# Stick-breaking attention in a macaron block: transposed weights made two groups at a time, their products with v further back, and the last pairs' results and output weights handled on other queues

## The chip, the cores and the metric

One core of a Trainium2 chip runs one program. The metric is the device time of one execution in microseconds (us); the time of a kernel is the median over several runs. The core has a matrix engine (PE), with its weight loads shown apart (PEld), a vector engine (DVE), an activation engine (ACT), GpSimd (POOL), and a queue engine (SP) that here issues the DMAs. Each engine runs its own instructions strictly in the order in which they stand in the program, and waits at an instruction whose operands or buffers are not ready.

## The reference, cut to what matters

The block is: half a SwiGLU feed-forward layer, attention, half a SwiGLU layer, each on an RMS-normalised x, for 1024 frames of 1024 features. Everything in the change lies in the attention.

```python
def stick_breaking_attention(xn, w_qkv, q_gain, k_gain, w_o):
    qkv = (xn @ w_qkv).reshape(b, s, 3, SB_HEADS, SB_HEAD_DIM)      # 16 heads of 64
    q = rms_norm(qkv[:, :, 0], q_gain); k = rms_norm(qkv[:, :, 1], k_gain); v = qkv[:, :, 2]
    for blk in range(s // Q_BLOCK):                                 # 8 blocks of 128 frames
        z = einsum('bhqd,bhkd->bhqk', q[:, :, lo:hi], k[:, :, :hi]) / sqrt(SB_HEAD_DIM)
        mask = s_idx < t_idx
        log_1m = where(mask, log_sigmoid(-z), 0.0)
        rev_excl = (sum of log_1m over the later keys of the row)
        w = where(mask, exp(log_sigmoid(z) + rev_excl), 0.0)
        outs.append(einsum('bhqk,bhkd->bhqd', w, v[:, :, :hi]))
    return concatenate(outs) @ w_o
```

The frames come in reversed, so that the running product over later keys becomes a scan from left to right.

## The kernel before, in words

The program has three long stretches: the first feed-forward layer, the attention with its output projection, and the second feed-forward layer. Matrix products in full precision are made as three products of a high and a low part (`mm3`, lines L308 to L310: high by high, high by low, low by high). A tensor is split into its two parts by `split`: ACT copies the high part out (L196), and DVE, or POOL where a caller says so, subtracts it from the tensor to get the low part (L197).

The attention works on eight pairs of heads (`p` = 0 to 7), which follow each other in time. While a pair is worked on, the q, k and v of the next pair are computed as filling work (`qkv`, 24 steps of nine or six matmuls with 384 columns into the PSUM banks `bq`). For a head `hd` and a half of the frames (`half` 1 is blocks 4 to 7, `half` 0 blocks 0 to 3) there are two kinds of work:

- `scores(state, hd, half)`: for each block `tb` of 128 query frames and each half `kb` of the keys, two matmuls make z in one of three banks `bz` (L1058), ACT takes two sigmoids from it (L1062), DVE runs a scan over one of them, which gives the running product (L1066), and POOL multiplies the scan into the other (L1073). The result is a tile w (`w03` is head 0, block 3 of its half). A bank `bz` comes free when its scan has read it. `prep_q` and `prep_k`, which turn q and k (L1016) and split them (L1020, L1021), use the same three banks.
- `values(state, p, hd, half)`: w is needed with the keys on the partitions. For each group (a block `sb` of 128 keys; the last group holds two blocks) `turn` transposes up to four 128 x 128 pieces of w into one of two banks `bt` (L1095), and `split` takes them out into a tile `th` (ACT) and a tile `tl` (DVE), of which there are two each. `apply` then multiplies v by `th` and by `tl` into the bank `bo` (L1113). A bank `bt` comes free when `tl` is written, a slot of `th` and `tl` when its product has read it. There are three groups for half 1 and seven for half 0. After the last group the sum is taken out into the tile `o`; after the second head, pairs 0 to 6 split `o` into two tiles `w12` and `w13`, store both to DRAM (`o_keep`, L1127), and `load_o` brings them back into `xh` and `xl` once the x that these hold is no longer read; pair 7 writes into `xh` and `xl` at once.

A pair's time is cut into four parts, a, b, c and d. The table `UNITS` says which scores a part makes, and `BEFORE` which earlier scores it applies: part a scores head 1 half 1 and applies head 0 half 1; b scores head 0 half 0 and applies head 1 half 1; c scores head 1 half 0 and applies head 0 half 0; d scores the next pair's head 0 half 1 and applies head 1 half 0.

The order on the engines comes from a list `plan` of (time, function). The times are the author's own units, used for sorting only; the functions are called in that order, and each call gives its instructions the next priorities. A scheduler that knows which instructions wait for which then lays out each engine's fixed order by priority, and can put a ready instruction ahead of one that it expects to wait. Before, group i of a part with `span` units was turned at

```python
t = TURN + (span - TURN) * i / len(groups)        # TURN = 4.0
put(part, t, to_turn)
put(part, t + APPLY, to_apply)                    # APPLY = 2.3
```

In the last pair there is no next qkv. Its place is taken by `project`: parts of the output projection for the first half of the columns (table `SHARES`, matmuls named `bq<-raw,xh` and the like). The weights w_o come in two halves of four loads each (`out_weights`, L1248): the loads go to two `raw` tiles in turn, so a load waits until the tile's earlier content is split. Which engine subtracts is set by `ON_POOL` for the first half (`wo0` to `wo2` POOL, `wo3` DVE); the second half was all on DVE.

Of the kernel before, what the change touches and what calls it, by code (L numbers as in the profile page):

```python
# [17 lines left out]
P = 128  # L18
# [15 lines left out]

ON_POOL = {"wo0", "wo1", "wo2"}

# [17 lines left out]

TURN, APPLY = 4.0, 2.3
RAW = 6
# [57 lines left out]
def macaron_kernel(ctx, tc, x, g1, w1_in, w1_out, gm, w_qkv, gq, gk, w_o, g2, w2_in, w2_out, out):  # L114
# [801 lines left out]
    with ExitStack() as stack:  # L916
# [121 lines left out]
        def scores(state, hd, half):  # L1038
# [3 lines left out]
            def step(tb, kb):  # L1042
# [29 lines left out]
                c1 = max(c0, 1)  # L1072
                pool_e.tensor_tensor(wt[:, c1 : c0 + n], wt[:, c1 : c0 + n], om[:, c1 - 1 : c0 + n - 1], op=ALU.mult)  # L1073

            return [partial(step, tb, kb) for tb in range(half * 4, half * 4 + 4) for kb in range(half, 2)]

        def values(state, p, hd, half):
# [5 lines left out]
            def blocks(sb):  # L1083
                return min(4, sb - tb0 + 1)

            def turn(sbs):
                w = state["w", hd, half]
                tp = bank("bt")
                n = 0
                for sb in sbs:  # L1090
                    for i in range(max(blocks(sb), 2)):
                        c = (sb - tb0 - i) * P

                        src = w[tb0 + i][:, c : c + P] if i < blocks(sb) else first[:, P : 2 * P]
                        pe.transpose(tp[:, n : n + P], src, ident)  # L1095
                        n += P
                th, tl = now[sbs] = [pl["th"].tile([P, NHALF], F32R, name=n) for n in ("th", "tl")]
                split(tp[:, :n], th[:, :n], tl[:, :n])

            def apply(sbs):  # L1100
# [18 lines left out]
                dve.tensor_tensor(o[own, :], ot[own, :], o[own, :], op=ALU.add)  # L1119
                if hd == 1 and p < NP - 1:  # L1120

                    oh, ol = (
                        pl["w"].tile([P, T - i * P], F32R, name=f"w1{i}", bufs=1)[:, :NHALF] for i in (2, 3)
                    )
                    split(o, oh, ol)
                    for to, src in zip(o_keep, (oh, ol)):
                        sp.dma_start(to[rows(p), HALVES[half]], src.bitcast(F32))  # L1127
                elif hd == 1:
                    split(o, xh[:, p, HALVES[half]], xl[:, p, HALVES[half]])
# [4 lines left out]
        def load_o(half):  # L1134

            for i in range(NP - 1):
                for to, src in zip((xh, xl), o_keep):
                    sp.dma_start(to[:, i, HALVES[half]].bitcast(F32), src[rows(i), HALVES[half]])


        states = [{} for _ in range(NP)]
# [35 lines left out]
        for p in range(-1, NP):  # L1177
# [9 lines left out]
            for part, span in PARTS.items():  # L1187
# [3 lines left out]
                if this is not None:  # L1191
                    groups = values(this, p, *BEFORE[part])
                    for i, (to_turn, to_apply) in enumerate(groups):
                        t = TURN + (span - TURN) * i / len(groups)
                        put(part, t, to_turn)
                        put(part, t + APPLY, to_apply)
            if nxt is not None:
                if p >= 0:
                    fills = qkv(p + 1, nxt)
                    for part, span in PARTS.items():  # L1200
                        for i in range(FILLS[part]):
                            put(part, (span - (3.0 if part == "d" else 0.0)) * (i + 0.5) / FILLS[part], fills.pop(0))
                put("c", 15.0, partial(prep_q, nxt, 1))
                put("c", 17.5 if p >= 0 else 20.0, partial(prep_k, nxt, 0, 1))
                put("d", 8.0, partial(prep_k, nxt, 1, 1))
            if this is not None:
                put("a", 5.0, partial(prep_q, this, 0))
                put("a", 7.5, partial(prep_k, this, 0, 0))
                put("b", 8.0, partial(prep_k, this, 1, 0))
            if 0 <= p < NP - 2:  # L1210
# [30 lines left out]
    with pools(*PROJECTION) as pl:  # L1241
# [3 lines left out]
        def out_weights(c, k, rooms):  # L1245
# [7 lines left out]
            if c is HALVES[0] and k < 6:  # L1253

                there = seen[:, k // 2 : k // 2 + 1] if k < 4 else wo[-1][1][:, 0:1].bitcast(F32)
                pool_e.tensor_tensor((l_ if k < 4 else h_)[:, 0:1], there, there, op=ALU.mult)
            split(raw, h_, l_, lane(f"wo{k // 2}") if c is HALVES[0] else dve)
            return [(h_[:, s], l_[:, s]) for s in HALVES]
# [108 lines left out]
```

## Time and profile before

| | us |
|---|---|
| median of 3 runs (lowest to highest) | 1930.62 (1930.38 to 1931.1) |
| the profiled execution | 1931.22 |
| its span in the trace | 1929.4 |
| PE busy | 1906.1 (99% of the span) |
| PEld, DVE, ACT, POOL busy | 1623.1, 1237.0, 978.5, 1115.7 |
| attention with its qkv and the first part of the projection | about 686 to 1240 of the span |
| mean granted PE clock | 1.0 of full speed |

How to read it: matmuls overlap, since the next one starts while the last one drains, and the ends in the trace are modelled. So "busy" hides short waits of PE. What a wait costs is read from the starts: the distance from one matmul's start to the next one's, less the usual distance for that size. Times are counted from the start of the span. Idle time on an engine that nobody waits for costs nothing.

### The profile page before, as it was taken

The numbers are of one execution on the slowest core, as the hardware profiler recorded it, in microseconds if no ns is written. First come the engines' busy times: TensorE is split into PE (matmuls) and PEld (weight loads), VectorE is DVE, ScalarE is ACT, GpSimd is POOL, SyncE is SP. The second block draws the span as 40 slices with busy tenths as digits, with TensorE's granted clock in tenths as the row PEclk, the third lists the DMA queues.
The fourth block names the chain that finished last, engine by engine and source line by source line (L and its number), as shares of the span: only waits on it lengthen the run. The fifth ranks groups of instructions, "written<-read, shape, count | busy, mean of one in ns | idle before, by whom it ended". The sixth has DMA issues, their size and how long they took to land.

```text
span 1929.4 us, 26653 instructions
## 1 busy us (share of the span) xinstructions
PE 1906.1 (99%) x9362; PEld 1623.1 (84%) x9362; DVE 1237.0 (64%) x1714; ACT 978.5 (51%) x1794; POOL 1115.7 (58%) x994
## 2 busy tenths in 40 slices
PE   9999999999999999999999999999999999999999
PEld 8878888888888899898989897788888888888887
DVE  6855455536775667887787778477455545548645
ACT  6433433343335467777787777344433443334332
POOL 5766667656456646655665564114667667655554
PEclk9999999999999999999999999999999999999999
DMA  6233323238996401111101144511323323369973
GB/s 202 88 120 105 104 87 126 94 118 294 347 321 234 134 25 45 39 39 45 45 31 48 50 143 141 197 55 59 116 88 125 100 97 104 121 212 341 336 268 139
DMA packets 169558, 259.70 MB, mean 135 GB/s; under 512 B 11728, under 2 KB 82384, under 8 KB 169424
## 3 DMA queue, kind: packets, MB, share of 16 engines
q1 hardware_dynamic: 169280, 258.00, 39.2%
q8 instruction: 73, 1.20, 0.3%
q14 instruction: 61, 0.50, 0.1%
q10 hardware_dynamic: 144, 0.00, 0.0%
HBM read 197.66 MB, written 60.29 MB: 134 GB/s over the span
## 4 chain that ended last, share of the span: by engine, by line
PE 85%; DVE 7%; ACT 2%; POOL 2%; issue 2%; DMA 1%; SPq 0%; DVEq 0%; POOLq 0%; ACTq 0%
PE ka L308 6%; PE ka L310 6%; PE ka L309 6%; PE kc L308 4%; PE kc L310 4%; PE kc L309 4%; PE bq L309 4%; PE bq L308 4%; PE bq L310 4%; PE kb L308 4%; PE ma L309 4%; PE ma L310 4%; PE kb L310 4%; PE ma L308 4%; PE kb L309 4%; PE bo L1113 3%
## 5 line engine op out<-in xcount | busy, mean ns | idle before, releaser
L197 POOL TENSOR_TENSOR rp<-raw,rp 128x1024 fp32r<-128x1024 f32 x84 | 212.5, 2534 | 169.9 <-ACT rp L196 159.1
L197 POOL TENSOR_TENSOR u<-sf,u 128x512 fp32r<-128x512 f32 x160 | 227.4, 1423 | 136.4 <-ACT u L196 136.4
L197 POOL TENSOR_TENSOR u<-raw,u 128x512 fp32r<-128x512 f32 x128 | 186.2, 1457 | 157.9 <-ACT u L196 157.1
L196 ACT ACTIVATE u<-sf 128x512 fp32r<-128x512 f32 x160 | 100.8, 630 | 204.9 <-PE kb L309 86.9
L1073 POOL TENSOR_TENSOR w<-w,om 128x512 f32<-128x512 f32 (+4 forms) x128 | 140.8, 1104 | 110.2 <-DVE om L1066 83.9
L446 DVE TENSOR_TENSOR h<-h 128x512 f32<-128x512 f32 x110 | 135.4, 1235 | 85.7 <-POOL h L554 85.0
L196 ACT ACTIVATE rp<-rh 128x1024 fp32r<-128x1024 f32 (+1 forms) x78 | 76.5, 984 | 196.6 <-PE mb L309 59.2
L308 PE MATMUL bq<-wqh,xh 128*128 128x384 f32 x512 | 174.5, 341 | 0.0
L310 PE MATMUL bq<-wqh,xl 128*128 128x384 f32 x512 | 172.2, 336 | 0.0
L309 PE MATMUL bq<-wql,xh 128*128 128x384 f32 x512 | 172.0, 336 | 0.0
L576 DVE TENSOR_TENSOR raw<-raw 128x1024 f32<-128x1024 f32 (+1 forms) x60 | 89.9, 1500 | 109.8 <-DMA raw<-w_out 94.9
L196 ACT ACTIVATE u<-raw 128x512 fp32r<-128x512 f32 x128 | 80.3, 630 | 151.6 <-PE ka L309 100.9
L308 PE MATMUL ka<-xh,u 128*128 128x512 f32 x352 | 137.2, 390 | 1.9 <-ACT s L499 1.9
L308 PE MATMUL ma<-rp 128*128 128x512 f32 x352 | 137.0, 389 | 0.0
L310 PE MATMUL ka<-xh,u 128*128 128x512 f32 x352 | 137.0, 389 | 0.0
L310 PE MATMUL ma<-rp 128*128 128x512 f32 x352 | 136.9, 389 | 0.0
L309 PE MATMUL ka<-xl,u 128*128 128x512 f32 x352 | 136.9, 389 | 0.0
L309 PE MATMUL ma<-rp 128*128 128x512 f32 x352 | 136.9, 389 | 0.0
L1062 ACT ACTIVATE w<-bz,f 128x512 f32<-128x512 f32 (+2 forms) x192 | 112.7, 587 | 42.2 <-PE bz L1058 39.4
L554 POOL TENSOR_TENSOR h<-h,g 128x512 f32<-128x512 f32 x80 | 112.9, 1411 | 35.4 <-DVE h L503 33.6
L475 DVE TENSOR_TENSOR sf<-raw 128x512 f32<-128x512 f32 x80 | 80.3, 1003 | 77.9 <-POOL u L197 77.9
L197 DVE TENSOR_TENSOR rp<-rh,rp 128x1024 fp32r<-128x1024 f32 (+1 forms) x70 | 110.8, 1600 | 22.1 <-ACT rp L196 19.6
(309 smaller groups left out, 5497.1 us busy)
## 6 DMA issues: line engine op xcount, KB each, us to landing
raw<-w_out SPq DMA_DIRECT2D x120, 512.0 KB, 5.7
raw<-w_in SPq DMA_DIRECT2D x86, 512.0 KB, 3.6
k<-h SPq DMA_DIRECT2D x154, 256.0 KB, 2.1
rh<-k SPq DMA_DIRECT2D x64, 512.0 KB, 6.3
raw_qkv<-w_qkv SPq DMA_DIRECT2D x64, 192.0 KB, 3.0
x_keep<-x SPq DMA_DIRECT2D x32, 256.0 KB, 3.7
x<-x_keep SPq DMA_DIRECT2D x32, 256.0 KB, 5.4
raw<-w_out SPq DMA_DIRECT2D x24, 256.0 KB, 3.6
```

Of the source, the lines that this page charges most:

```text
L196: first = act.activation(hi, raw, AF.Copy).ins
L197: return first, (engine or dve).tensor_tensor(lo, raw, hi.bitcast(F32), op=ALU.subtract).ins
L308: pe.matmul(dst, ah, bh, start=start and i == 0, stop=False, skip_group_check=onto)
L309: pe.matmul(dst, ah, bl, start=False, stop=False, skip_group_check=onto)
L310: pe.matmul(dst, al, bh, start=False, stop=stop and i == n - 1, skip_group_check=onto)
L446: dve.tensor_tensor(src, hb[of[0]], hb[of[1]], op=getattr(ALU, of[2]))
L475: dve.tensor_tensor(f[n], x, y, op=op)
L554: pool_e.tensor_tensor(h, h, gs[k], op=ALU.mult)
L576: dve.tensor_tensor(w[0], w[0], w[1], op=getattr(ALU, W_OF[m][2]))
L1062: marks["scored"] = act.activation(to, z, AF.Sigmoid, scale=state["f", half][:, sign, tb % 4, hd : hd + 1]).ins
L1073: pool_e.tensor_tensor(wt[:, c1 : c0 + n], wt[:, c1 : c0 + n], om[:, c1 - 1 : c0 + n - 1], op=ALU.mult)
L1113: pe.matmul(ot[:, :n], vv, t[:, c : c + n], start=start, stop=stop)
```

## The change

It leaves every product and its operands as they were, and moves work in order and between engines and queues:

- `TURN` becomes a number per part (a 4.0, b 4.0, c 7.5, d 5.0), `APPLY` 3.3 where it was 2.3, and the groups are turned in twos: groups 0 and 1 at one time, 2 and 3 at the next.
- All transposes of a group get the priority of its first one, so that they stay together where they are ready.
- In parts c and d of the last pair `turn` and `apply` are given a priority 12 later.
- `prep_k` for head 1 half 0 moves from 8.0 to 10.7 of part b, and the last qkv step of part a comes 0.1 earlier.
- The store of `o` needs one `w` tile (`w13`) and no longer two: the low part is written over `o` itself. Pair 6 stores half 1 only; its half 0 goes into `xh` and `xl` at once, and `load_o` fetches six rows, not seven, for half 0.
- `wo3` is subtracted on POOL. For the second half of w_o the copies on ACT follow the last sigmoid that was emitted, and the subtractions are cut in two halves of 512 columns; of its four loads the first two are subtracted on POOL, behind the last product of w (`marks["weighed"]`), the other two on DVE.

```diff
-ON_POOL = {"wo0", "wo1", "wo2"}
+ON_POOL = {"wo0", "wo1", "wo2", "wo3"}
-TURN, APPLY = 4.0, 2.3
+TURN, APPLY = {"a": 4.0, "b": 4.0, "c": 7.5, "d": 5.0}, 3.3
 ...
             def turn(sbs):
-                n = 0
+                n, now_at = 0, tc.cur_priority
 ...
+                        tc.cur_priority = now_at
                         pe.transpose(tp[:, n : n + P], src, ident)
 ...
-                if hd == 1 and p < NP - 1:
-                    oh, ol = (
-                        pl["w"].tile([P, T - i * P], F32R, name=f"w1{i}", bufs=1)[:, :NHALF] for i in (2, 3)
-                    )
+                if hd == 1 and (p < NP - 2 or p == NP - 2 and half):
+                    oh = pl["w"].tile([P, T - 3 * P], F32R, name="w13", bufs=1)[:, :NHALF]
+                    ol = o.bitcast(F32R)
 ...
-            for i in range(NP - 1):
+            for i in range(NP - 2 + half):
 ...
+        def behind(f, n=12):
+            with sooner(-n):
+                f()
 ...
-                        t = TURN + (span - TURN) * i / len(groups)
+                        t = TURN[part] + (span - TURN[part]) * (i - i % 2) / len(groups)
+                        if p == NP - 1 and part in "cd":
+                            to_turn, to_apply = partial(behind, to_turn), partial(behind, to_apply)
 ...
-                put("b", 8.0, partial(prep_k, this, 1, 0))
+                put("b", 10.7, partial(prep_k, this, 1, 0))
 ...
-            split(raw, h_, l_, lane(f"wo{k // 2}") if c is HALVES[0] else dve)
+            if c is HALVES[0]:
+                split(raw, h_, l_, lane(f"wo{k // 2}"))
+            else:
+                with following(marks["scored"] if k < 4 else None):
+                    act.activation(h_, raw, AF.Copy)
+                with following(marks["weighed"] if k < 4 else None):
+                    for s in HALVES:
+                        engine = pool_e if k < 4 else dve
+                        engine.tensor_tensor(l_[:, s], raw[:, s], h_[:, s].bitcast(F32), op=ALU.subtract)
```

The order on the engines, at three places. First, ACT at the start of part c of a middle pair (`th` is the high part of a turned group, `w` and `bz` after L1062 are the two sigmoids of a score; the 128x384 score is that of block 1). Before:

```order
L980 ACTIVATE sq<-bq 128x256
L981 ACTIVATE qk_9888<-bq 128x256
L984 ACTIVATE vst<-bq 128x2x64
L196 ACTIVATE th<-bt 128x512 x2
L207 ACTIVATE rs_a<-ssq 128x16
L1062 ACTIVATE w_10279<-bz,f_9833 128x384
L1062 ACTIVATE bz<-bz,f_9833 128x384
L196 ACTIVATE th<-bt 128x512
L1062 ACTIVATE w_10279<-bz,f_9833 128x512
```

The same place after the change:

```order
L984 ACTIVATE vst<-bq 128x2x64
L1062 ACTIVATE w_10248<-bz,f_9834 128x384
L1062 ACTIVATE bz<-bz,f_9834 128x384
L207 ACTIVATE rs_a<-ssq 128x16
L196 ACTIVATE th<-bt 128x512 x2
L1062 ACTIVATE w_10248<-bz,f_9834 128x512
L1062 ACTIVATE bz<-bz,f_9834 128x512
L196 ACTIVATE th<-bt 128x512 x2
```

The first two groups now stand behind the first score of block 1, where they stood ahead of it, and the next two stand together. On PE their transposes stand nine qkv matmuls and that score further back.

Second, PE in part a of a middle pair (`bo` is the product with v, `bt` a transpose, `bz<-ident,qk` the turning of k, `bz<-kh_s` a score). Before:

```order
L1113 MATMUL bo<-th,vst 128x512
L1113 MATMUL bo<-tl,vst 128x512
L1016 MATMUL bz<-ident,qk_9446 128x128 x4
L1095 MATMUL bt<-ident,w_9657 128x128
L1095 MATMUL bt<-ident,w_9705 128x128
L1095 MATMUL bt<-ident,w_9657 128x128
L1095 MATMUL bt<-ident,first 128x128
L1113 MATMUL bo<-th,vst 128x384
L1113 MATMUL bo<-tl,vst 128x384
L1058 MATMUL bz<-kh_s_9736,q_s_9563 128x256
L1058 MATMUL bz<-kl_s_9737,q_s_9563 128x256
L308 MATMUL bq<-wqh,xh 128x384
```

The same place after the change:

```order
L1113 MATMUL bo<-th,vst 128x512
L1113 MATMUL bo<-tl,vst 128x512
L1113 MATMUL bo<-th,vst 128x384
L1113 MATMUL bo<-tl,vst 128x384
L1016 MATMUL bz<-ident,qk_9417 128x128 x4
L1098 MATMUL bt<-ident,w_9650 128x128
L1098 MATMUL bt<-ident,w_9698 128x128
L1098 MATMUL bt<-ident,w_9650 128x128
L1098 MATMUL bt<-ident,first 128x128
L308 MATMUL bq<-wqh,xh 128x384
L309 MATMUL bq<-wql,xh 128x384
L310 MATMUL bq<-wqh,xl 128x384
```

The two products with v follow each other, and the score of 256 columns that stood right behind them now stands behind nine qkv matmuls; the product of the third group stands behind that score, the first score of part b and nine more.

Third, POOL where pair 7 begins (`wd` and `wc` are the low parts of the last two loads of the first half of w_o, the rest are the products of w of blocks 5, 6 and 7). Before:

```order
L1073 TENSOR_TENSOR w_12234<-w_12234 128x383
L197 TENSOR_TENSOR wd<-raw,wa 128x1024
L1071 MEMSET w_12296 128x1
L1073 TENSOR_TENSOR w_12296<-w_12296 128x255
L1071 MEMSET w_12359 128x1
L1073 TENSOR_TENSOR w_12359<-w_12359 128x127
```

The same place after the change:

```order
L1073 TENSOR_TENSOR w_12221<-w_12221 128x383
L197 TENSOR_TENSOR wd<-raw,wa 128x1024
L197 TENSOR_TENSOR wc<-raw,wb 128x1024
L1071 MEMSET w_12281 128x1
L1073 TENSOR_TENSOR w_12281<-w_12281 128x255
L1071 MEMSET w_12344 128x1
L1073 TENSOR_TENSOR w_12344<-w_12344 128x127
```

The subtraction `wc` has come from DVE and stands ahead of the products of blocks 6 and 7. The four halves of `wf` and `wh` have come too; they stand behind the last product of pair 7.

More of the change, by code (lines that the diff above doesn't have):

```diff
@@ L1072, in step @@
                 c1 = max(c0, 1)
-                pool_e.tensor_tensor(wt[:, c1 : c0 + n], wt[:, c1 : c0 + n], om[:, c1 - 1 : c0 + n - 1], op=ALU.mult)
+                marks["weighed"] = pool_e.tensor_tensor(
+                    wt[:, c1 : c0 + n], wt[:, c1 : c0 + n], om[:, c1 - 1 : c0 + n - 1], op=ALU.mult
+                ).ins
             return [partial(step, tb, kb) for tb in range(half * 4, half * 4 + 4) for kb in range(half, 2)]
@@ L1201, in macaron_kernel @@
                         for i in range(FILLS[part]):
-                            put(part, (span - (3.0 if part == "d" else 0.0)) * (i + 0.5) / FILLS[part], fills.pop(0))
+                            t = (span - (3.0 if part == "d" else 0.0)) * (i + 0.5) / FILLS[part]
+                            put(part, t - 0.1 if (part, i) == ("a", FILLS["a"] - 1) else t, fills.pop(0))
                 put("c", 15.0, partial(prep_q, nxt, 1))
```

## The prediction, as it went on record

> **What bounds the kernel now.** I read the head of the page first, then the chain that ended last, then the busy time by stretches, then who PE waited for, and last the rows of PE in one pair.
>
> ```profile
> span 1929.4 us, 26653 instructions
> PE 85%; DVE 7%; ACT 2%; POOL 2%; issue 2%; DMA 1%; SPq 0%; DVEq 0%; POOLq 0%; ACTq 0%
> ```
>
> PE holds 85% of the chain. So time comes back only where PE stands still. The stretches (length, then busy time and count of PE, PEld, DVE, ACT and POOL, the clock, the DMA share) show where that can be: 686 to 1125 holds pairs 0 to 6, 1125 to 1240 the last of pair 6 and pair 7.
>
> ```profile
> 686.00:1125.00 439.00, 431.14 (x2599) 397.92 (x2598) 346.40 (x666) 342.71 (x749) 250.65 (x382) 1.00 0.13 41
> 1125.00:1240.00 115.00, 109.28 (x584) 89.56 (x583) 84.78 (x137) 71.04 (x141) 49.29 (x69) 1.00 0.46 151
> ```
>
> PE idles 7.9 us in the first and 5.7 us in the second, and DVE and ACT have about a fifth of their time free in the first (346 and 343 of 439), so neither is a second bound there. The 13.6 us are the least that the waits cost, since a modelled end covers the start of each wait. Who is waited for, from 684 to 1236 (total, times, longest):
>
> ```profile
> PE bt L1095 <- POOL w L1071: 4.7, 8, 0.6
> ...
> PE bz L1058 <- DVE w L1066: 2.4, 8, 1.1
> ...
> PEld bo L1113 <- DVE tl L197: 14.6, 41, 1.2
> ```
>
> Three kinds recur: a transpose that waits for POOL's product of w, a score that waits for its bank `bz`, and a product with v that waits for `tl`. The change touches all three.
>
> **Part c: the first transposes.** In each of seven pairs the chain goes from PE to a product on POOL and back; the first and the last:
>
> ```profile
> 731.34 1.63 POOL w L1073
> ...
> 1124.37 1.64 POOL w L1073
> ```
>
> One of them on PE:
>
> ```profile
> 993.86 0.49 PE L1095 MATMUL bt<-ident,w 128*128 128x128 f32 x3
> 994.99 0.77 PE L1095 MATMUL bt<-ident,w 128*128 128x128 f32 x5 [0.64 <-POOL w L1071]
> 995.51 0.42 PE L1058 MATMUL bz<-kh_s,q_s 128*128 128x384 f32 x1
> ```
>
> Transposes start about 0.11 apart (five in the 0.52 to the score). Three starting at 993.86 end their steps at 994.19; the fourth, which reads the last block's w, starts at 994.99. The cost is 0.80 (the 0.64 shown and what the modelled end hides). In the new order these transposes stand nine qkv matmuls and a score of 384 columns later, 1.9 us by the steps below, over twice the wait. The scores ahead of them don't move, so POOL's product doesn't come later. Gain 7 x 0.80 = 5.6.
>
> **Part a: bank and `tl`.** The rows of PE of one pair:
>
> ```profile
> 1037.28 0.41 PE L1113 MATMUL bo<-tl,vst 128*128 128x384 f32 x1
> 1037.84 0.39 PE L1058 MATMUL bz<-kh_s,q_s 128*128 128x256 f32 x1 [0.15 <-DVE w L1066]
> 1038.06 0.28 PE L1058 MATMUL bz<-kl_s,q_s 128*128 128x256 f32 x1
> 1038.18 0.34 PE L308 MATMUL bq<-wqh,xh 128*128 128x384 f32 x1
> 1038.36 0.34 PE L309 MATMUL bq<-wql,xh 128*128 128x384 f32 x1
> ...
> 1039.86 0.40 PE L1058 MATMUL bz<-kh_s,q_s 128*128 128x512 f32 x1
> 1040.54 0.39 PE L1113 MATMUL bo<-tl,vst 128*128 128x256 f32 x1 [0.28 <-DVE tl L197]
> 1040.76 0.28 PE L1113 MATMUL bo<-th,vst 128*128 128x256 f32 x1
> ...
> 1042.81 0.39 PE L1058 MATMUL bz<-kh_s,q_s 128*128 128x512 f32 x1
> 1043.04 0.40 PE L1058 MATMUL bz<-kl_s,q_s 128*128 128x512 f32 x1
> ```
>
> Usual steps from start to start: 384 columns 0.18, 256 columns 0.12, 512 columns 0.23. Here 1037.28 to 1037.84 is 0.56, 0.38 too long; the next step 0.22, 0.10 too long (PE starts again slowly after a wait); 1039.86 to 1040.54 is 0.68, 0.45 too long; the next 0.10 again. Together 1.03. In the new order the score of 256 columns comes nine qkv matmuls (1.6) later, and the product that waited for `tl` comes behind that score, one of 512 columns and nine more qkv matmuls: 1.6 + 0.2 + 0.5 + 1.6 = 3.9 behind its transposes. These now stand two products ahead of 1037.28, so `tl` needs some 3.5 (to 1040.54). Both waits are covered, the second by 0.4. Six pairs: 6.2.
>
> **The end of part b, and the other waits for `tl`.**
>
> ```profile
> 1054.32 0.28 PE L1113 MATMUL bo<-th,vst 128*128 128x256 f32 x1
> 1054.59 0.38 PE L1113 MATMUL bo<-tl,vst 128*128 128x256 f32 x1
> 1054.81 0.28 PE L1113 MATMUL bo<-th,vst 128*128 128x256 f32 x1
> ...
> 1003.16 0.40 PE L1113 MATMUL bo<-th,vst 128*128 128x512 f32 x1
> 1003.51 0.51 PE L1113 MATMUL bo<-tl,vst 128*128 128x512 f32 x1
> ```
>
> 0.27 and 0.22 stand where 0.12 is usual: 0.25 lost. The turning of k (four transposes) and a score of 512 columns come between, 0.9 more, so seven pairs give 1.8. In part c 1003.16 to 1003.51 is 0.12 too long. Of the 41 waits for `tl` thirteen are counted above; I take 25 of the others (the rest is the last pair's) at 0.12, 3.0, with nothing and 0.23 (a restart of 0.11 with each) as ends, 0 to 5.8. They go because a product now follows its transposes 3.3 units later in the plan and not 2.3.
>
> **What two at a time costs.** There are two banks `bt` and two slots of `th` and `tl`. A second two can be turned while the first two wait for their products, but not taken out.
>
> ```profile
> 1033.18 0.60 PE L1095 MATMUL bt<-ident,w 128*128 128x128 f32 x4
> ...
> 1033.88 0.60 ACT L196 ACTIVATE th<-bt 128x512 fp32r<-128x512 f32 x1
> ...
> 1035.16 0.67 DVE L197 TENSOR_TENSOR tl<-bt,th 128x512 fp32r<-128x512 f32 x1
> ...
> 1020.55 1.62 ACT L948 ACTIVATE wqh<-raw_qkv 128x768 fp32r<-128x768 f32 x2
> ```
>
> ACT starts 0.70 after the first of four transposes, takes 0.6, DVE 0.67. Part d is tightest: its third two needs the banks of the second two, whose `th` waits for the first two's products to have read their slots. From the start of the first group's product with `tl`: 0.4 until it is read, 0.6 and 0.7 for ACT and DVE, some 0.2 of handing over, 1.9; 0.6 more for the second group, 2.5. PE has until then that product (0.2), the next two (0.5), nine qkv matmuls (1.6) and a score (0.2), 2.5 to the first four transposes and 0.4 more to the next: margins of 0.6 and 0.4. ACT's two copies (1.62 together) stand just ahead in its order; they start 1.3 before the slot comes free, so they could eat 0.3 of it. I charge 0.2 per pair, 1.3 in all; ends 0 and 1.6 per pair (both copies late). Elsewhere at least 1.6 of qkv work lies between. The transposes' new priority, the qkv step 0.1 earlier and `prep_k` later cost nothing by themselves: no product is added, and `prep_k`'s bank has a score's whole time (1.6 of qkv) to come free. The store of `o` has as many DMAs as before, and SP loses one fetch and one store pair in pair 6; nothing on PE reads those rows that early.
>
> **The last pair.** It has little filling work, so DVE and POOL count. From the chain (start, length), then rows of PE, then of POOL:
>
> ```profile
> 1156.08 2.31 DVE wc L197
> ...
> 1172.62 1.21 DVE wf L197
> ...
> 1192.83 0.72 DVE wh L197
> ```
>
> ```profile
> 1158.28 0.48 PE L1113 MATMUL bo<-th,vst 128*128 128x512 f32 x1
> 1159.62 0.51 PE L1113 MATMUL bo<-tl,vst 128*128 128x512 f32 x1 [0.86 <-DVE tl L197]
> ...
> 1214.16 0.27 PE L1095 MATMUL bt<-ident,w 128*128 128x128 f32 x1
> 1215.67 0.33 PE L1095 MATMUL bt<-ident,w 128*128 128x128 f32 x1 [1.23 <-POOL w L1073]
> ```
>
> ```profile
> 1154.90 2.40 POOL L197 TENSOR_TENSOR wd<-raw,wa 128x1024 fp32r<-128x1024 f32 x1 [1.56 <-issue]
> ...
> 1159.07 0.72 POOL L1073 TENSOR_TENSOR w<-w 128x255 f32<-128x255 f32 x1 [1.73 <-DVE w L1066]
> ```
>
> Three subtractions for w_o lie on the chain on DVE and leave it. `wc` holds up `tl`: 1159.62 less 1158.28 is 1.34, 1.11 too long. `wf` and `wh` give 1.21 and 0.72 of chain. Part d's first transposes stand still for 1.51 less 0.11, 1.40; they move behind more projection work. Sum 4.4. Against it: `wc` on POOL ends at 1154.90 + 2.40 + 2.40 = 1159.7, 0.6 after the product of block 6 begins now, so that is 0.6 later. And at the end, where no qkv work is left and four groups stand in a row, each two can wait for slots: by the 1.9 and 2.5 above against some 1.6 of projection work, 0.3 to 0.9; I take 1.0 with a restart. Net gain 2.8. The ends are a loss of 2.4 (below), and 10.5: the 5.7 idle and 0.16 hidden in each of some 30 waits.
>
> The Trainium skill's "GPSIMD Engine Reference", section "Engine selection", says that elementwise work with two inputs belongs on VectorE, since GpSimd is about twice as slow. The rows agree for the length: 2.40 on POOL, 1.21 for `wf` on DVE. By that rule alone moving these three would be a mistake; yet `wc` took 2.31 on DVE while POOL ran `wd`, and it is the queue that counts.
>
> **The sum.** 5.6 + 6.2 + 1.8 + 3.0 - 1.3 + 2.8 = 18.1. The profiled execution took 1931.2 (1.8 around its span), 0.6 above the median shown; 1930.6 - 18.1 gives 1912.5, and I say 1912.
>
> **The rivals.**
> - POOL becomes the bound of the last pair (chance 0.20). `wc`'s 2.4 lie wholly ahead of the products of blocks 6 and 7, and nothing that leaves DVE helps PE. For it: PE does wait for POOL there (1.23 above), and POOL's chain into part b has no filling work. Against: block 6's product waits 1.73 for DVE now. Then the last pair loses 2.4 and the other pairs keep 15.3: 1917.7. This is what the skill's rule would give.
> - Waits only change their place (0.08): scores come no earlier, and what PE saves at a transpose it stands before the next scan. Against: DVE and ACT have a fifth of their time free. Between 1927 and 1934, 1930.5.
> - Slower (0.06): in parts c and d the two slots don't come free in time, because ACT's copies of the qkv weights stand ahead of `th`. With 1.6 at three double turns a pair that is 4.8 against the 2.3 that a pair gains (15.3 over six and a half): + 2.5 x 6, 1945. It decides from 0.29 at each of the eight double turns of a pair.
>
> **How the numbers follow.** The forecast has 0.66. Its own range, from the ends above, is 1902 (all waits for `tl` with restarts, 2.8 more, and the last pair's 10.5 where 2.8 are counted) to 1921 (1.6 per pair in part d and not 0.2). POOL's case lies in it and reaches 1922.5 if the waits for `tl` worth 3.0 and 1.8 stay. I give 1902 to 1923; two in ten lie outside: the last two rivals and ends of the others. About 0.2%, 3.9 us, is what a measurement of this kernel can tell from none. Faster: 0.66 + 0.20 = 0.86; same 0.08; slower 0.06.
>
> **What would show it.** Right: the seven POOL products leave the chain and PE's waits for POOL's w fall from 8 to one or two; PE's waits for `bz` go except at pair 0's start; PEld's waits for `tl` fall from 41 to under 15; PE's idle time from 686 to 1125 falls from 7.9 to under 2.5; a pair takes about 63.2 us, where POOL's rows on the chain now stand 65.5 apart (1124.37 less 731.34, by six). Wrong: PE waits for `bt` behind DVE's `tl` in part d, or the last 115 us get longer with POOL's `wc` or a raw w_o load on the chain.

## The result, and the profile after

The changed kernel takes 1914.43 us (median of 5 runs, 1914.03 to 1914.58) against 1931.1 (1930.38 to 1931.55) of the kernel before on the same chip: 16.7 us less, a ratio of 0.9913 with a 95% interval of 0.9900 to 0.9927. The forecast was 1912 (1902 to 1923). It is 2.4 above the forecast, and the sum of 18.1 us was 1.4 too large; the terms of that sum were further off than the sum, as the parts below show.

The head of the page and the chain of the changed kernel: POOL's share of the chain fell from 2% to 1%, and of the seven products of w on POOL that stood in it from 731 to 1125 us, 1.63 each, none is left.

```profile
span 1912.5 us, 26698 instructions
PE 86%; DVE 8%; ACT 3%; issue 1%; POOL 1%; DMA 0%; SPq 0%; DVEq 0%; ACTq 0%; POOLq 0%
```

Busy time by stretches (length, then PE, PEld, DVE, ACT, POOL, clock, DMA share, GB/s). The first row is the stretch that the forecast named. The second starts 13 us earlier than the forecast's second stretch, at about the same place of the work; the last product with v, which began at 1232.7, now begins at 1217.5, so the row holds some more of what follows:

```profile
686.00:1125.00 439.00, 435.45 (x2658) 408.47 (x2657) 354.52 (x687) 352.21 (x768) 260.49 (x395) 1.00 0.15 47
...
1112.00:1227.00 115.00, 112.83 (x607) 94.79 (x606) 83.24 (x139) 72.62 (x144) 61.18 (x76) 1.00 0.49 162
```

PE stands idle for 3.6 us where it was 7.9, and for 2.2 where it was 5.7. Who it waits for, from 684 to 1236 us (total, times, longest), PE first, then its weight loads:

```profile
PE bz L1058 <- DVE kl_s L1021: 1.5, 7, 0.2
PE bz L1016 <- POOL w L1071: 0.9, 1, 0.9
PE bz L1058 <- DVE w L1066: 0.9, 3, 0.3
PE bo L1116 <- DVE tl L197: 0.6, 1, 0.6
...
PE bt L1098 <- POOL w L1073: 0.2, 1, 0.2
...
PEld bo L1116 <- DVE tl L197: 6.8, 22, 1.0
PEld bz L1058 <- DVE kl_s L1021: 3.7, 7, 0.5
PEld bq L308 <- DVE f L1003: 3.4, 7, 0.5
```

The eight waits of transposes for POOL's product are down to one of 0.2, those for `bz` from 8 to 3, those for `tl` from 41 to 22. Two rows were not there before: seven times, once in each pair, a score waits for `kl_s` and a qkv matmul for `f`.

To say where the time went I use ACT's copies `kh_s`, of which each pair has four, always at the same places of the work. Four of them are shown: the first of all, the one in part a of pair 0, that in part a of pair 5, and the last one in part c of pair 6, which lies 16 us behind the 1125 us of the forecast. Before, then after:

```profile
694.83 0.69 ACT L1020 ACTIVATE kh_s<-bz,gk_sb 128x512 fp32r<-128x512 f32 x1 [2.67 <-PE bz L1016]
711.47 0.69 ACT L1020 ACTIVATE kh_s<-bz,gk_sb 128x512 fp32r<-128x512 f32 x1
1038.19 0.69 ACT L1020 ACTIVATE kh_s<-bz,gk_sb 128x512 fp32r<-128x512 f32 x1
1141.06 0.69 ACT L1020 ACTIVATE kh_s<-bz,gk_sb 128x512 fp32r<-128x512 f32 x1 [0.55 <-PE bz L1016]
```

```profile
693.68 0.69 ACT L1020 ACTIVATE kh_s<-bz,gk_sb 128x512 fp32r<-128x512 f32 x1 [2.67 <-PE bz L1016]
710.25 0.69 ACT L1020 ACTIVATE kh_s<-bz,gk_sb 128x512 fp32r<-128x512 f32 x1
1027.72 0.69 ACT L1020 ACTIVATE kh_s<-bz,gk_sb 128x512 fp32r<-128x512 f32 x1
1128.39 0.69 ACT L1020 ACTIVATE kh_s<-bz,gk_sb 128x512 fp32r<-128x512 f32 x1 [0.17 <-PE bz L1016]
```

A fifth of the stretch from the second row to the third is the period of a pair: 65.34 before, 63.49 after. From the first row to the last ("the pairs" from here on) is 446.2 and 434.7, so 11.5 us came from there. From the last row to the end of the span (1929.4 and 1912.5) is 788.3 and 784.1: 4.2 came from the end of pair 6 and from pair 7. The spans differ by 16.9, and the remaining 1.2 lie ahead of the first row, where no work was changed; that row stands between 693.4 and 695.0 in all fourteen kernels, so I take it for the spread of single executions. The same numbers for every kernel:

| kernel | period | the pairs | from there to the end | median |
|---|---|---|---|---|
| before | 65.34 | 446.2 | 788.3 | 1931.1 |
| turning edits only | 63.94 | 436.1 | 786.3 | 1918.56 |
| output-weight edits only | 65.70 | 447.9 | 788.6 | 1929.7 |
| part c's turn later only | 65.19 | 444.9 | 786.8 | 1927.29 |
| store edits only | 65.03 | 444.8 | 789.1 | 1929.57 |
| c's turn and every product later only | 64.48 | 443.5 | 789.5 | 1928.0 |
| turning and store | 63.53 | 435.0 | 785.5 | 1916.52 |
| turning and output weights | 64.05 | 436.8 | 784.6 | 1917.33 |
| after | 63.49 | 434.7 | 784.1 | 1914.43 |
| after, one group at a time | 63.77 | 437.2 | 784.2 | 1916.78 |
| after, part c's turn at 4.0 again | 64.16 | 439.6 | 783.6 | 1918.52 |
| after, part b's first score later | 63.62 | 436.1 | 784.1 | 1914.69 |
| the same, and b's first products later | 63.03 | 431.4 | 784.3 | 1911.9 |
| the same, and one fill of part c later | 62.93 | 430.7 | 784.0 | 1910.57 |

The kernel before had medians of 1930.4 to 1931.1 beside these runs, so differences of medians between groups of runs carry up to 0.7 us. The stretches of the table don't carry that, but each is of one profiled execution: for the output-weight edits it was the longest of ten (1932.37), and one wait of 2.1 for a store, 1.1 in the kernel before, is in its pairs. What PE lost in the pairs, by cause, is worked out from all its rows there: each step from start to start, less the usual one (0.11 for a transpose; 0.12, 0.17 and 0.23 for 256, 384 and 512 columns), put down to what the late instruction, or its weight load, waited for, with the slow step behind it counted to the same cause (us). The row of `tl` has many short waits; counting only those that made PE late by over 0.03 gives 0.4 to 1.2 less in it:

| PE waits for | before | c later only | after | singles | c at 4.0 | b's score | b's products | c's fill |
|---|---|---|---|---|---|---|---|---|
| POOL's w (`bt`) | 5.9 | 0 | 0 | 0 | 0 | 0 | 0 | 0 |
| DVE's w (`bz`) | 5.4 | 5.6 | 1.1 | 1.1 | 1.1 | 1.1 | 1.1 | 1.1 |
| `tl` | 9.6 | 14.0 | 4.0 | 4.5 | 10.7 | 8.3 | 4.0 | 5.6 |
| `kl_s` | 0 | 0 | 3.4 | 3.3 | 3.4 | 0 | 0 | 0 |
| `f` | 0 | 0 | 2.3 | 4.4 | 0 | 2.4 | 2.3 | 0 |
| all, with the small ones | 24.5 | 23.5 | 13.4 | 15.8 | 17.6 | 14.8 | 10.1 | 9.4 |

(In columns from the left: the kernel before, the run with c's turn alone, the changed kernel, and it with one group at a time, with c at 4.0, and the three steps of the last part of the experiments.)

### The profile page after: what moved, and what is told of

It reads as the page before. It is cut to its first block, busy times and chain, and to the rows that moved or that the text cites. A ratio compares the mean times of both kernels' runs of the same rounds, so it can differ in the third digit from the quotient of the medians.

```text
span 1912.5 us, 26698 instructions
## 1 busy us (share of the span) xinstructions
PE 1897.4 (99%) x9362; PEld 1624.8 (85%) x9362; DVE 1237.0 (65%) x1713; ACT 979.9 (51%) x1794; POOL 1127.8 (59%) x999
## 4 chain that ended last, share of the span: by engine, by line
PE 86%; DVE 8%; ACT 3%; issue 1%; POOL 1%; DMA 0%; SPq 0%; DVEq 0%; ACTq 0%; POOLq 0%
PE ka L308 6%; PE ka L309 6%; PE ka L310 6%; PE bq L308 4%; PE bq L309 4%; PE bq L310 4%; PE kc L308 4%; PE kc L309 4%; PE kc L310 4%; PE ma L310 4%; PE ma L309 4%; PE ma L308 4%; PE kb L308 4%; PE kb L309 4%; PE kb L310 4%; PE mb L310 3%
## 5 line engine op out<-in xcount | busy, mean ns | idle before, releaser
L576 DVE TENSOR_TENSOR raw<-raw 128x1024 f32<-128x1024 f32 (+1 forms) x60 | 95.0, 1585 | 105.4 <-DMA raw<-w_out 91.7
L1062 ACT ACTIVATE w<-bz,f 128x512 f32<-128x512 f32 (+1 forms) x192 | 113.1, 589 | 34.5 <-PE bz L1058 33.4
```

The source lines that it names most:

```text
L576: dve.tensor_tensor(w[0], w[0], w[1], op=getattr(ALU, W_OF[m][2]))
L1062: marks["scored"] = act.activation(to, z, AF.Sigmoid, scale=state["f", half][:, sign, tb % 4, hd : hd + 1]).ins
```

## The experiments: parts of the change alone

**The turning edits alone**, in the kernel before (every hunk of the diff on `TURN`, `APPLY`, `turn`, `behind`, the twos, the qkv step and `prep_k`; none on the store and the output weights).

> The kernel before with the turning edits alone (TURN by part, APPLY 3.3, groups in twos, transposes kept together, prep_k of part b later, the last pair's c and d put back); stores and output weights as before. Theory, the waits of PE inside the pairs are what the change removes: 1915 to 1918, the seven waits of 0.8 us for POOL's product in part c gone, most of the gain of 16.7 here. Rival, the gain comes from DVE's and SP's relief in the last pair: above 1924.

1918.56 us (1917.85 to 1919.19), ratio 0.9936 (0.9921 to 0.9951). The theory's range was missed by half a microsecond; the rival's was not reached. So 12.0 of 16.7 us are the turning's. No run tried the smaller turning edits singly: the transposes kept together, `prep_k` later, the qkv step earlier, the last pair's priorities.

**The output-weight edits alone**: `ON_POOL` with `wo3`, `marks["weighed"]` and the split cut in halves.

> The kernel before with the output-weight edits alone (wo3 subtracted on POOL, the second half cut in two, its first two loads on POOL behind the last product of w). Theory, the subtractions on DVE's queue were on the chain of the last pair: 2 to 3 us less, 1928 to 1929, the wait of 1.1 us for tl at 1159 gone. Rival, POOL becomes late for its products of w: 2.4 us more, 1933 or above.

1929.7 us (1928.93 to 1932.37), ratio 0.9996 (0.9986 to 1.0005): no change that can be measured, and neither the theory's time nor the rival's. The wait that the theory named did go: at its place the product with `tl` starts 0.32 behind the one with `th` (1159.19 and 1159.51), where it was 1.34. But the stretch behind the pairs is no shorter (788.6 against 788.3), so what it gained was lost again there; where, no run here tried.

**The turn of part c alone:**

```diff
-TURN, APPLY = 4.0, 2.3
+TURN, APPLY = {"a": 4.0, "b": 4.0, "c": 7.5, "d": 4.0}, 2.3
-                        t = TURN + (span - TURN) * i / len(groups)
+                        t = TURN[part] + (span - TURN[part]) * i / len(groups)
```

> The kernel before with one number changed: the groups of part c are turned from 7.5 and not from 4.0; APPLY 2.3 and one group at a time as before. Theory, the wait for the last block's product is simply a too early place: 7 x 0.8 = 5.6 us less, 1925 to 1926. Rival, the seven groups crowded into the rest of part c wait for their banks and tl instead: 1930 or more, with more waits of PEld for tl than 41.

1927.29 us (1926.99 to 1928.52), ratio 0.9984 (0.9975 to 0.9993): 3.3 us, of which the pairs hold 1.3. The waits for POOL's product are gone, 5.9 us, as expected, but those for `tl` grew from 9.6 to 14.0. PE in one pair now reads

```profile
998.32 0.28 PE L1058 MATMUL bz<-kl_s,q_s 128*128 128x256 f32 x1
998.44 0.34 PE L308 MATMUL bq<-wqh,xh 128*128 128x384 f32 x1
999.44 0.51 PE L1113 MATMUL bo<-tl,vst 128*128 128x512 f32 x1 [0.66 <-DVE tl L197]
999.79 0.34 PE L309 MATMUL bq<-wql,xh 128*128 128x384 f32 x1
```

998.44 to 999.44 is 1.00 where a step of 384 columns takes 0.18: 0.82 lost, as much as the 0.80 that part c's transposes had lost. The transposes moved nearer to the product that reads them, and the wait moved from the one to the other.

**The store edits alone** (one tile `w13`, the low part over `o`, pair 6's half 0 not stored).

> The kernel before with the edits of the store of o alone (one w tile, the low part over o itself, pair 6's half 0 straight into xh). Theory: within 1 us of before, 1930 to 1931.5; only the one longer wait of part a at 905.7 (1.3 where the others have 0.4) shrinks, since there a score waited for a store to leave its w tile. Rival, the stores hold up part a in every pair: 3 us less or more.

1929.57 us (1929.01 to 1930.52), ratio 0.9994 (0.9985 to 1.0003): 1.0 less than the kernel before beside it, at the edge of the theory's "within 1 us" and 0.4 below its range. The one wait that the theory named went. In the kernel before, ACT once stands, at the turn from pair 2 to pair 3, for a tile that a store still reads:

```profile
905.59 0.47 ACT L1062 ACTIVATE w<-bz,f 128x256 f32<-128x256 f32 x1 [1.76 <-DMA o_keeph<-w]
```

From part a of pair 2 to part a of pair 3 that kernel takes 66.53 us, for the pairs on both sides 65.2 and 65.0; with the store edits it takes 65.16. The second `w` tile held for the store was worth 1.3 us, once.

**Part c's turn and every product later**, one group at a time: the diff of the last but one with 3.3 in place of 2.3.

> The kernel before with two numbers alone: part c's first turn at 7.5 and every product 3.3 behind its turn in place of 2.3; one group at a time. Theory: the run with c's turn alone lost its gain since the first product of part c then stood too close behind its split (0.8 us of waiting for tl in each pair, from none); with the product one step further back that wait goes, and the pair falls from 65.0 to 64.2 or less: 1920 to 1923. Rival: with one group at a time the products only meet tl's split later in the queue of DVE, and nothing is gained over the late turn alone: 1926 to 1928.

1928.0 us (1925.2 to 1929.5 in 11 runs), ratio 0.9985 (0.9976 to 0.9994). The waits for `tl` went as the theory said, from 14.0 with the late turn alone to 3.6. Four of the six steps from pair to pair come near to its 64.2 (64.1 to 64.6), but the time does not follow: from part a of pair 5 to that of pair 6 it is 68.8 us, and there are new waits for `q_s` (4.6) and `f` (4.4). PE stands for 3.3 us at one place in pair 5, and the rows say why:

```profile
1088.72 1.06 ACT L196 ACTIVATE raw<-raw 128x1024 fp32r<-128x1024 f32 x1 [3.05 <-DMA raw<-w_o]
...
1090.31 0.45 PE L1113 MATMUL bo<-th,vst 128*128 128x384 f32 x1 [3.11 <-ACT th L196]
```

ACT takes its work in order, stood 3.05 us at the first split of w_o for the load, and the copy `th` that PE needed was behind it. A second loss lies behind the pairs, in a stretch of 789.5 where the late turn alone has 786.8: there PE once stands 2.1 us for the turning of q and k, which waits for POOL, where that run stands 0.5. So what the later products gained is given back at these two places and in the new waits. The run's wide spread fits a wait for a DMA, though no run here tried that.

## The experiments: the changed kernel with one part undone

**One group at a time:**

```diff
-                        t = TURN[part] + (span - TURN[part]) * (i - i % 2) / len(groups)
+                        t = TURN[part] + (span - TURN[part]) * i / len(groups)
```

> The changed kernel with its groups turned one at a time again (the times of part c, of part d, the products 3.3 behind, the last pair's priorities and the other edits stay). Theory, from the kernel with the turning edits alone (1918.6, where turning part c later alone gave 3.3 of 12 us) : it is the turning by twos that removes the waits of the products for tl, since two groups' splits then lie behind eight transposes and a fill; without it the PE rows of bo waiting for tl come back in parts a to d, about 0.5 to 0.9 us a pair: 1918 to 1921. Rival: the later product (3.3 in place of 2.3) does this alone, and the twos are worth nothing: 1913.5 to 1915.5.

1916.78 us (1916.5 to 1917.03): 2.35 more than with twos, between the two theories. At one product in a pair the wait for `tl` is 0.27, and the wait for `f` takes 0.63 with the step behind it where it took 0.31:

```profile
992.75 0.40 PE L1116 MATMUL bo<-th,vst 128*128 128x512 f32 x1
993.25 0.50 PE L1116 MATMUL bo<-tl,vst 128*128 128x512 f32 x1
...
994.26 0.40 PE L1058 MATMUL bz<-kl_s,q_s 128*128 128x512 f32 x1
995.01 0.44 PE L308 MATMUL bq<-wqh,xh 128*128 128x384 f32 x1 [0.36 <-DVE f L1003]
```

So the twos, which the change is named after, are worth 2.35 of its 16.7 us by the medians, 2.5 by the pairs; the waits for `tl` stay away without them (4.5 against 4.0), so it is the later products, with the rest of the turning, that removed these. What the twos took away is about half of the wait for `f` (4.4 against 2.3).

**Part c's turn at 4.0 again:**

```diff
-TURN, APPLY = {"a": 4.0, "b": 4.0, "c": 7.5, "d": 5.0}, 3.3
+TURN, APPLY = {"a": 4.0, "b": 4.0, "c": 4.0, "d": 5.0}, 3.3
```

> The changed kernel with part c's first turn at 4.0 again, as in the kernel before. Theory: part c's first transposes wait for POOL's product again, 0.8 us in each of 7 pairs as in the kernel before: plus 5.6, 1919 to 1921, with seven rows of PE bt waiting for POOL w. Rival, from the run in which the late c alone gave 3.3 us because the products behind it then waited 0.8 for tl: the place of the turn trades one wait for another, and the change of c's time is worth 0 to 3: 1914 to 1917.5.

1918.52 us (1918.36 to 1918.63), 4.1 more, nearest to the theory's number, with another wait than the theory's. No row of transposes waiting for POOL came back: POOL starts the product 1.22 ahead of the first transpose here (921.51 and 922.73) and not 0.59 as in the kernel before (928.10 and 928.69), and takes 1.29 for it and not 1.63. So the other edits cover that wait even without the later turn. PE waits 0.72 at a product with v instead, here with DVE's rows behind it:

```profile
925.54 0.40 PE L1116 MATMUL bo<-th,vst 128*128 128x512 f32 x1
926.49 0.50 PE L1116 MATMUL bo<-tl,vst 128*128 128x512 f32 x1 [0.55 <-DVE tl L197]
```

```profile
924.04 1.28 DVE L1066 TENSOR_TENSOR_SCAN om<-bz,om,first 128x512 f32<-128x512 f32 x1
...
925.75 0.68 DVE L197 TENSOR_TENSOR tl<-bt,th 128x512 fp32r<-128x512 f32 x1
```

`tl` stands on DVE behind a scan of 1.28 and two small steps, in one unbroken row. Together with the run that moved c's turn alone this is the main finding: the same edit is worth 1.3 us in the pairs of the kernel before and 4.9 in those of the changed one. It pays there only where the products stand far enough back. That alone is not enough: with the later products but none of the other edits the late turn gained nothing more (1928.0). The medians differ less, 3.3 and 4.1, since behind the pairs the late turn gains 1.5 in the one kernel and loses 0.5 in the other.

**Turning and store; turning and output weights**, each in the kernel before.

> The kernel before with the turning edits and the store edits, without those of the output weights. The turning edits alone gave 1918.6 and a steady pair of 63.84 us, all edits together 1914.4 and 63.50. Theory: the 0.3 us a pair is the store's (the split of o in place frees its buffers sooner and changes the order of DVE at the end of part a), the rest, near 1.9, is the output weights' in the last pair: pair of 63.5, 1916 to 1917. Rival: the store is worth nothing here either, as it was alone (1 us): 1918 to 1919.

> The kernel before with the turning edits and those of the output weights, without the store's. Theory: pair of 63.84 as with the turning alone, and some 1.9 us less in the last pair, where the splits of the output weights leave the queues of DVE: 1916 to 1917. Rival: the output weights alone gave 0.9 us and are worth no more here: 1917.5 to 1919.

1916.52 us (1916.49 to 1917.26) and 1917.33 (1917.17 to 1918.58). The first came as its theory said, with a period of 63.53. So the output weights are worth 2.1 us in company (1916.52 less 1914.43), 1.4 of it behind the pairs. The second lies 0.3 above its theory's range and 0.2 below its rival's, so it decides for neither. By it the store is worth 2.9 in company (1917.33 less 1914.43), 2.1 of it in the pairs. Alone the two gave 0.9 and 1.0, which can't be told from nothing.

## The experiments: where the rest of the pair's waits went

**Part b's first score behind the next fill.** In the changed kernel PE waits for `kl_s`, then starts slowly:

```profile
965.43 0.40 PE L1058 MATMUL bz<-kh_s,q_s 128*128 128x512 f32 x1
966.03 0.50 PE L1058 MATMUL bz<-kl_s,q_s 128*128 128x512 f32 x1 [0.20 <-DVE kl_s L1021]
966.37 0.34 PE L308 MATMUL bq<-wqh,xh 128*128 128x384 f32 x1
```

965.43 to 966.03 is 0.37 too long, the next step 0.11. The edit:

```diff
+                    steps = scores(state, *UNITS[part])
+                    if part == "b":
+                        put(part, 1.2, steps[0])
+                        steps = steps[1:]
-                    spread(scores(state, *UNITS[part]), start[part], start[part] + span, 0.5)
+                    spread(steps, start[part] + (span / 8 if part == "b" else 0.0), start[part] + span, 0.5)
```

> The changed kernel with the first score step of part b put behind the qkv fill that follows it (nine matmuls of 128x384, some 1.57 us) in place of ahead of it; nothing else moves in the order of PE. Theory: the 0.37 + 0.11 us that PE waits there in each of 7 pairs for the copy kl_s go (it is 0.48 late, the fill covers 1.57) and no other wait takes their place: minus 3.4, 1910.5 to 1911.5. Rival: the scores of part b come 1.6 later to ACT, POOL and DVE, and the turns of part c wait for them instead: 1914 to 1917.

1914.69 us (1914.45 to 1915.56), the time that the rival gave, though not at its place. The seven waits for `kl_s` are gone, and each pair has a new one of 0.42 at part b's first products (`tl` from 4.0 to 8.3), not at part c's turns:

```profile
904.42 0.69 ACT L1062 ACTIVATE w<-bz,f 128x512 f32<-128x512 f32 x1 [1.43 <-PE bz L1058]
```

```profile
909.28 1.15 DVE L197 TENSOR_TENSOR tl<-bt,th 128x512 fp32r<-128x512 f32 x2
```

```profile
909.37 0.40 PE L1116 MATMUL bo<-th,vst 128*128 128x512 f32 x1
910.02 0.50 PE L1116 MATMUL bo<-tl,vst 128*128 128x512 f32 x1 [0.26 <-DVE tl L197]
```

ACT stands 1.43 for the late score, everything behind it in its order is later, `th` among it, and so DVE's `tl`.

**Part b's first products behind a fill too**, in that kernel:

```diff
-                        put(part, t + APPLY, to_apply)
+                        put(part, t + (4.5 if part == "b" and i < 2 else APPLY), to_apply)
```

> The changed kernel with the first score step of part b behind the next qkv fill, as in the run where that alone gave nothing, and now also the first two products of part b one fill (nine matmuls, 1.57 us) further back; on DVE and ACT the order is that of that run. Theory: in that run the wait for kl_s (0.48 a pair) only changed place to those products (0.42 + 0.10 + 0.06 of waiting for tl, since ACT was idle 1.43 us for the late scores and its copies th came after them); with the products behind a fill too, it goes: 7 x 0.5 less than the changed kernel, 1910.5 to 1912. Rival: the wait moves on once more, to part b's last products or to the read of the bank before part c: 1914 to 1915.5.

1911.9 us (1911.52 to 1912.26), ratio 0.9901 (0.9886 to 0.9917): the wait is gone, and the pair's period falls to 63.03. The chain shows it (two rows that are two pairs apart):

```profile
925.10 1.19 DVE om L1066
...
1051.15 1.19 DVE om L1066
```

**One fill of part c behind the products that followed it:**

```diff
-                            put(part, t - 0.1 if (part, i) == ("a", FILLS["a"] - 1) else t, fills.pop(0))
+                            put(part, t - 0.1 if (part, i) == ("a", FILLS["a"] - 1) else t + 0.5 if (part, i) == ("c", 5) else t, fills.pop(0))
```

> The last variant (part b's first scores and first products each behind a fill) with one more pair of neighbours exchanged on PE: in part c the qkv fill whose bank is held until f is read (0.2 + 0.1 us of waiting in each pair) stands behind the four products that followed it. ACT and DVE keep their order. Theory: f lies 0.4 us ahead of need then, but the second of those products needs its tl at 991.74 on that run's clock, when DVE ends it at 991.81: the wait changes place and shrinks from 0.31 to some 0.1 to 0.2, minus 0.7 to 1.5: 1910.4 to 1911.2. Rival: the wait for tl is as long as that for f was: 1911.5 to 1912.5.

1910.57 us (1910.17 to 1911.77), ratio 0.9895 (0.9879 to 0.9912), within the theory's range. The wait for `f` (0.2 + 0.1) is gone, one of 0.1 + 0.1 for `tl` stands in its place. The period falls by 0.1, 0.7 us in the pairs: `f` from 2.3 to nothing, `tl` from 4.0 to 5.6. This version beats both kernels: 3.9 us less than the changed one.

## Why the prediction was right, and which terms were mis-sized

**The waits that were named went, at nearly the price named.** The forecast had 5.6 for POOL's product: 5.9 went. It had 6.2 + 1.8 + 3.0 = 11.0 for the bank `bz` and for `tl`: 15.0 less 5.1 is 9.9. Single counts were less exact (22 weight loads still wait for `tl`, not under 15; PE idles for 3.6 in the stretch named, not under 2.5), and some of the 9.9 is the wait of ACT for the store in pair 3, to which no price was given.

**What took their place was mis-sized.** For new waits the sum had 1.3, for transposes in part d behind the slots of `th` and `tl`. These did not come: no transpose waits for `tl` in part d of these pairs, at the margins of 0.4 and 0.6 that were worked out; the list has two, both at the end of the last pair. Two other waits came, 5.7 us together, that stand in no term: `kl_s` 3.4 and `f` 2.3. They are most of the reason why the pairs gave 11.5 and not 15.3, and the period is 63.49 and not 63.2. Neither row was late before; PE comes to both earlier now. For `f` the rows are, DVE then PE:

```profile
992.27 0.68 DVE L197 TENSOR_TENSOR tl<-bt,th 128x512 fp32r<-128x512 f32 x1
992.88 0.15 DVE L992 TENSOR_SCALAR r<-bq 128x8 f32<-128x8 f32 x1
992.95 0.23 DVE L1003 TENSOR_SCALAR f<-bq 128x8 f32<-128x8 f32 x2
```

```profile
992.79 0.40 PE L1058 MATMUL bz<-kl_s,q_s 128*128 128x512 f32 x1
993.23 0.44 PE L308 MATMUL bq<-wqh,xh 128*128 128x384 f32 x1
```

The qkv matmul needs the bank that `f` is read from, and `f` stands behind a split on DVE. I had asked of each moved transpose and product what covers it, and not of the instructions that PE reaches earlier what they wait for.

**The 5.6 of part c is the price of all the turning edits, not of c's turn.** Moved alone, the turn gave 1.3 in the pairs; put back alone, it cost 4.9, and then at `tl` and not at POOL's product. Its cover was reckoned on the transposes' side and not on that of the products behind them, which the 3.3 had to move as well.

**The end gave 4.2 where 2.8 was the sum.** PE's losses from the last `kh_s` row to the end of the pairs fell from 9.9 to 5.0. The three subtractions for w_o left the chain, waits for `tl` fell from 3.0 to 0.2, and the stall of part d's first transposes, 1.39, is gone; those of part b wait 0.41 where they waited 1.01 and 0.30. The two charges against it were too large. The four groups in a row at the end wait 0.31 where 1.0 was charged; and `wc` stands on POOL so:

```profile
1141.75 2.40 POOL L197 TENSOR_TENSOR wd<-raw,wa 128x1024 fp32r<-128x1024 f32 x1 [0.67 <-POOL w L1073]
1144.10 2.41 POOL L197 TENSOR_TENSOR wc<-raw,wb 128x1024 fp32r<-128x1024 f32 x1
1146.50 0.75 POOL L1073 TENSOR_TENSOR w<-w 128x255 f32<-128x255 f32 x1
```

Block 6's product starts 2.40 after `wc`'s start, at once behind it, and no transpose waits for it. The longest wait left is 7 us further on, where the turning of q and k waits for POOL's products with r:

```profile
1153.61 0.49 PE L1098 MATMUL bt<-ident,w 128*128 128x128 f32 x3
1154.98 0.66 PE L1016 MATMUL bz<-ident,qk 128*128 128x128 f32 x4 [0.88 <-POOL w L1071]
```

```profile
1152.46 1.01 POOL L1073 TENSOR_TENSOR w<-w 128x383 f32<-128x383 f32 x1 [0.79 <-DVE bq L212]
1153.42 1.50 POOL L996 TENSOR_TENSOR qk<-qk,r 128x512 f32<-128x512 f32 x1
```

1.37 less 0.33 is 1.04, where the kernel before lost 0.54. The kernel with the turning alone, in which `wc` is still on DVE, loses 1.07 there, so it is not `wc` that causes it.

**In part luck.** That the sum came within 1.4 of the measured 16.7 rests on errors that offset each other: the pairs gave 3.8 less than their terms, the end 1.4 more, and of the 16.9 between the two spans 1.2 lie ahead of all that was changed.

**The rivals.** POOL as the bound of the last pair did not come (1917.7; that pair gained). Waits that only change place came when c's turn or b's score was moved alone; in the change itself two new waits took 5.7 us back, against 16 of old waits that went, and as a verdict on the whole (1930.5) it was wrong. The slots in part d cost nothing.

## What to carry to other kernels

When PE is fed by a chain of engines that take their work in order, price a moved instruction at both of its ends: what it waits for, and what stands behind it and is now nearer. Then ask of each wait that goes which is late next, to the bank and the small copy; here two rows that no list of waits showed before took back 5.7 of 16 us. Edits that fail alone can pay together (the late turn 1.3 or 4.9 in the pairs, the store 1 or 2.9, a score moved 0 and then, with its products, 2.5), so an edit that only moves a wait is to be followed to the place where the wait went and not dropped.

## What the runs showed of the hardware

A subtraction on DVE with both inputs in SBUF ran far longer while POOL worked, and an instruction of the same size with one input in PSUM (`bt`) did not. In the changed kernel, ahead of and then during four subtractions of POOL:

```profile
1219.50 0.69 DVE L1275 TENSOR_TENSOR wj<-raw,wi 128x512 fp32r<-128x512 f32 x1 [0.39 <-ACT wi L1271]
...
1222.71 0.68 DVE L1283 TENSOR_TENSOR x<-bt,x 128x512 f32<-128x512 f32 x1
...
1224.58 1.77 DVE L1275 TENSOR_TENSOR wl<-raw,wk 128x512 fp32r<-128x512 f32 x1
```

```profile
1221.53 5.96 POOL L197 TENSOR_TENSOR u<-raw,u 128x512 fp32r<-128x512 f32 x4 [18.37 <-ACT u L196]
```

The same form takes 0.69 and 1.77. Taken singly, POOL's four take 1.31, 1.32, 1.74 and 1.74. The third runs from 1224.06 to 1225.80: `wl` starts at 1224.58, and its 1.77 is 1.22 up to that end and 0.55 behind it. The `wc` of the forecast shows the same: it started at 1156.08 beside a `wd` that ended at 1154.90 + 2.40 = 1157.30, and its 2.31 is 1.22 up to that end and 1.09 behind it, where `wf` took 1.21 alone. The Trainium skill's "SBUF — State Buffer", section "Who interferes with whom", says that a DVE instruction with two SBUF inputs contends with a GpSimd instruction that reads SBUF. The Trainium skill's section "SBUF: two separate sides" on the same page says that whichever of the two starts first holds the shared ports for its whole instruction, and the other is blocked. These rows agree with both. So moving `wc` to POOL did not only trade 2.31 on DVE for 2.40 on POOL; it removed a collision. What that collision alone was worth in the kernel's time, no run here shows.
